# Row-Winograd convolution with max pool on Trainium2: last product in halves, stores image by image, and a new order

## The chip, the cores and the metric

The kernel runs on one core of a Trainium2 chip. The metric is the device time of one execution in microseconds (us), as the median of several runs. A core has five engines that run their own instruction streams and wait for each other by semaphores: TensorE (PE in the profile) for matrix products, VectorE (DVE), ScalarE (ACT), GpSimd (POOL) and SyncE (SP), which here only issues transfers. Sixteen DMA engines move data between the memory outside the core (DRAM) and the core's own memory (SBUF). Products are gathered in PSUM, which the kernel uses as eight banks.

## The reference, cut to what matters

```python
batch, c_in, h, w, c_out, k = 16, 64, 64, 64, 128, 3      # all float32
conv[b, co] += weight[co, ci, kh, kw] * x_pad[b, ci, kh:kh+h, kw:kw+w]   # pad 1, all ci, kh, kw
output[b, c, i, j] = max(conv[b, c, 2*i:2*i+2, 2*j:2*j+2])               # 16 x 128 x 32 x 32
```

A 3x3 convolution with padding 1, followed by a 2x2 maximum without overlap.

## The kernel before, in words

**The algorithm.** Each pooled row needs two rows of the convolution. The four input rows that they read are combined along the row axis, so that the two convolution rows are a + c and b + c with a common part c, and max(a + c, b + c) = max(a, b) + c. So c, the last product of every step, is added after the row maximum has been taken. The taps of the weights are combined the same way into seven blocks (`D2`, `G0`, `D0`, `G2`, `GM`, `G1`, `GP`), which are transposed once at the start.

**The tiling.** There are 32 steps. A step is two images (one on each half of the 128 partitions, numbered h = 0 and 1) and a quarter of the rows: 8 pooled rows of 64 columns for each image, which is 512 numbers on each of 128 output channels, one PSUM bank. The string `TYPES` gives each step one of two forms. A K step reads bf16 rows that a load on GpSimd's queue has cast (`kx`); it has the products PA1, PA2, PB1, PB2 and, last, PR. A W step reads fp32 rows (`wx`, loaded by SP) from which row differences E (`we`) and D (`wd`) and row sums WS (`ws`) are computed on POOL or DVE; it has the products P2, P0, P3 and, last, P1. A product has three matmuls, one for each column tap, for each image; `product` (line 272) collects the two images in `lanes` and emits their matmuls by turns. All emit from line 219 or, for the transposes, line 170.

**The steps between.** The code names them in the order string, each with the step and the image:
- SE, `seed` (copy at line 451, ACT): copies the first sum into the bank of the second, which then goes on from it.
- EV, `evac` (lines 439 and 441, ACT): moves the first sum to SBUF.
- MX, `rowmax` (line 467, DVE): maximum of the two rows, in PSUM. The last product (PR or P1) waits for it.
- OD, `odd` (line 471, ACT): copies the odd columns to SBUF after the last product.
- CM, `colmax` (line 477, DVE): maximum of even and odd columns into the output tile `o` (eight buffers); it gives the PSUM bank back.
- ST, `store` (lines 485 and 487): one store of 256 KB for both images on SP; for step 31 one store for each image, the first on ACT's queue.
- XC, `odd_rows` (line 335, ACT): puts odd rows of a W step into PSUM, so that WS reads them there (line 339). Other WS are a plain sum (line 360) or a reduction (line 352), by the step's place in `SUM_BY_REDUCTION`.
- E, `we` (line 372): on DVE for the steps in `DIFF_ON_VECTOR`, otherwise on POOL. D, `wd` (line 381): on POOL. KS (line 320): row sums of a K step, DVE.
- L (line 112, SP) and LK (line 101, POOL) are loads. LB is a load like L that is held until an earlier operation on DVE is done. The names of weights' blocks with T (transposes on PE) and V (copy of the transposed block to SBUF, on ACT for those in `TURNED_BY_SCALAR`, otherwise on DVE).
- The first K step and the first W step are in two row halves: F and G for their products, SEa/SEb, Ea/Eb, Da/Db; XOa, XOb, XEa, XEb cast the first rows, X1 and X2 the next.

**The order.** Nothing is scheduled by a planner. The string `ORDER` (lines 537 to 591) lists all steps of all engines, and a loop calls them one after the other; each engine executes its own in that order and the semaphores follow from the data. Banks are taken from a list `free` and given back to it in the same order, so the string also decides which bank a step gets. SP's transfers stand in this order too: a transfer that waits holds the ones behind it.

Of the kernel before, what the change touches and what calls it, by code (L numbers as in the profile page):

```python
# [11 lines left out]
def kernel(  # L12
# [460 lines left out]
    def colmax(s, h):  # L473
        if s not in ot:
            ot[s] = o_pool.tile([128, 2, R, WO], FP32, name="o")
        t = tb.pop((s, h))
        nc.vector.tensor_tensor(out=ot[s][:, h], in0=acc[t][:, :, 0::2], in1=od[s, h], op=MAX)  # L477
        free.append(t)

    def store(s, h=None):  # L480
        p, q = place[s]
        dst = out[2 * p : 2 * p + 2, :, q * R : (q + 1) * R, :].rearrange("b c h w -> c b (h w)")
        src = ot[s].rearrange("p b h w -> p b (h w)")
        if h is None:
            nc.sync.dma_start(out=dst, in_=src)
        else:
            (nc.scalar, nc.sync)[h].dma_start(out=dst[:, h : h + 1], in_=src[:, h : h + 1])

# [45 lines left out]
    for m in PRODUCTS:  # L534
# [18 lines left out]
        PA1.13.1 OD.8.1 PA2.13.1 L.19 EV.9.0 SE.11.0 CM.8.1 EV.13.1 L.24 D.12 P0.9.1 OD.8.0 P3.9.1 P2.12.1
        P0.11.0 P3.11.0 WS.11 PA1.10.1 PA2.10.1 MX.9.0 P1.9.0 EV.9.1 PA1.13.0 EV.11.0 ST.4 CM.8.0 XC.14 ST.2
        MX.9.1 OD.9.0 SE.12.1 MX.11.0 P1.9.1 P2.11.1 WS.14 PA2.13.0 P1.11.0 EV.10.1 P0.12.1 EV.13.0 PA1.10.0
        E.14 OD.9.1 CM.9.0 P2.14.0 OD.11.0 SE.11.1 WS.12 CM.9.1 EV.12.1 P3.12.1 P0.11.1 D.14 PB1.10.1 CM.11.0
        E.15 P3.11.1 PA2.10.0 E.19 SE.14.0 EV.11.1 P2.12.0 KS.10 MX.12.1 E.17 PB2.10.1 L.23 P1.12.1 P0.14.0
        SE.12.0 MX.11.1 P1.11.1 P3.14.0 EV.14.0 XC.22 MX.14.0 EV.10.0 P0.12.0 WS.22 P2.14.1 MX.10.1 ST.1 P3.12.0
        E.20 EV.12.0 P1.14.0 OD.14.0 MX.12.0 PB1.13.1 OD.12.1 OD.11.1 PB1.10.0 CM.14.0 PB2.10.0 ST.6 P1.12.0
        CM.12.1 PB2.13.1 E.16 CM.11.1 PR.10.1 SE.14.1 P0.14.1 PA1.21.0 MX.13.1 ST.11 XC.17 PR.13.1 OD.12.0  # L560
        OD.10.1 P3.14.1 EV.14.1 PA2.21.0 MX.10.0 OD.13.1 CM.12.0 P2.15.1 EV.21.0 PR.10.0 D.15 D.16 P2.15.0
        CM.10.1 WS.17 CM.13.1 PA1.18.0 MX.14.1 PA2.18.0 OD.10.0 SE.15.0 P2.16.1 CM.10.0 WS.16 WS.15 P0.15.0
        SE.15.1 P3.15.0 SE.16.1 P1.14.1 PB1.13.0 EV.18.0 P0.15.1 OD.14.1 EV.15.0 P0.16.1 P3.15.1 KS.18 EV.15.1
        LK.2.0 CM.14.1 P2.16.0 ST.12 MX.15.0 ST.14 MX.15.1 P3.16.1 D.17 P2.17.1 EV.16.1 P1.15.1 PB2.13.0 MX.16.1
        SE.16.0 SE.17.1 P1.16.1 P1.15.0 P0.17.1 OD.15.0 P0.16.0 L.28 L.25 MX.13.0 P3.17.1 OD.15.1 EV.16.0
        PR.13.0 PA1.18.1 OD.16.1 P3.16.0 OD.13.0 D.20 WS.20 CM.15.1 EV.17.1 PA2.18.1 P2.17.0 CM.16.1 MX.16.0
        SE.17.0 P2.20.1 CM.13.0 P2.19.0 MX.17.1 EV.18.1 P1.17.1 P1.16.0 P0.17.0 CM.15.0 P3.17.0 OD.16.0 SE.20.1
        PA1.21.1 PB1.18.0 EV.17.0 SE.19.0 CM.16.0 ST.9 WS.19 OD.17.1 D.19 P0.20.1 EV.20.1 PA2.21.1 PB2.18.0
        MX.17.0 MX.18.0 E.24 P0.19.0 E.22 P3.20.1 P1.17.0 P2.19.1 EV.21.1 EV.19.0 CM.17.1 PR.18.0 PB1.18.1 E.23
        P3.19.0 MX.20.1 OD.17.0 OD.18.0 P2.20.0 ST.8 P1.20.1 SE.19.1 WS.23 OD.20.1 CM.17.0 P2.23.0 CM.18.0  # L570
        PB2.18.1 MX.19.0 SE.20.0 P1.19.0 L.30 P0.19.1 MX.18.1 EV.19.1 D.23 P3.19.1 OD.19.0 CM.20.1 KS.21 P0.20.0
        D.22 PR.18.1 P2.22.1 SE.23.0 P3.20.0 ST.10 CM.19.0 MX.19.1 PB1.21.1 EV.20.0 MX.20.0 OD.18.1 P0.23.0
# [65 lines left out]
```

## Time and profile before

| | |
|---|---|
| median of 3 runs | 104.52 us (104.48, 104.52, 104.57) |
| the profiled execution | 104.47 us; its span in the trace 102.7 us |
| granted clock of TensorE | 1.0 throughout |
| PE busy | 96.2 us, 94% of the span |
| DVE busy | 91.6 us, 89% |
| ACT busy | 85.5 us, 83% |
| POOL busy | 77.9 us, 76% |
| moved by DMA | 23.60 MB: 17.14 MB read and 8.39 MB written in DRAM |

The span is what the profile shows between the first and the last instruction; the execution's own time is 1.81 us longer. The costliest groups after the matmuls are the row differences D on POOL (2360 ns each), the row maxima on DVE (691 ns each, 64 of them), the seeds and evacuations on ACT (591 to 614 ns) and the column maxima on DVE (416 ns, 64 of them).

A line of the page's section 5 gives the line of code, the engine, the operation, the tiles, their shape and the count, and then the busy time with the mean of one. A name with q behind an engine (SPq) is its queue, which waits and issues. In section 2 each digit is a tenth of the busy share in one fortieth of the span.

### The profile page before, as it was taken

How to read it: one execution, taken by the hardware profiler on the slowest of the kernel's cores; microseconds unless marked ns; L12 is line 12 of the kernel's file. 1: busy time of each engine (PE TensorE's matmuls, PEld its weight loads, DVE VectorE, ACT ScalarE, POOL GpSimd, SP SyncE). 2: the span in 40 equal slices, each digit the busy share in tenths (PEclk: the TensorE clock that was granted, in tenths of full speed). 3: DMA queues.
4: the chain of work that ended last, by engine and by line, in shares of the span. 5: the costliest groups of instructions: out<-in, count | busy, mean ns of one | idle time of the engine just before them, and what ended most of it. 6: DMA issues, size and time to landing. Idle time of an engine off the chain costs nothing.

```text
span 102.7 us, 2522 instructions
## 1 busy us (share of the span) xinstructions
PE 96.2 (94%) x905; PEld 54.3 (53%) x905; DVE 91.6 (89%) x176; ACT 85.5 (83%) x192; POOL 77.9 (76%) x66
## 2 busy tenths in 40 slices
PE   6969999999999999999999999999999999999920
PEld 2355465444454447655655555567657765555500
DVE  1576979999999999999999989999999999899960
ACT  4278697999889999997998899897989899897830
POOL 6262889995998799489959999789999688990000
PEclk9999999999999999999999999999999999999999
DMA  2989999999999999600538989930803673386553
GB/s 53 286 295 333 281 325 360 362 421 410 293 311 410 311 308 396 220 6 0 175 57 119 245 259 404 389 111 0 307 3 112 216 165 113 106 295 222 208 192 114
DMA packets 13341, 23.60 MB, mean 230 GB/s; under 512 B 1040, under 2 KB 9360, under 8 KB 13328
## 3 DMA queue, kind: packets, MB, share of 16 engines
q1 hardware_dynamic: 12464, 21.20, 58.8%
q0 software_dynamic: 720, 2.10, 11.6%
q8 instruction: 7, 0.11, 0.5%
q10 hardware_dynamic: 144, 0.13, 0.4%
q14 instruction: 6, 0.05, 0.1%
HBM read 17.14 MB, written 8.39 MB: 249 GB/s over the span
## 4 chain that ended last, share of the span: by engine, by line
PE 88%; DMA 4%; DVE 2%; SPq 1%; issue 1%; ACT 0%; DVEq 0%
PE acc L219 86%; DMA kfirst<-in_x_dram 4%; DVE o L477 1%; PE acc L170 1%; DVE acc L467 1%; PE acc L460 1%; SPq L119 0%; ACT kx L492 0%; SPq L115 0%; DVEq L633 0%
## 5 line engine op out<-in xcount | busy, mean ns | idle before, releaser
L219 PEld LDWEIGHTS <-wt 64*128 64x128 bf16 x870 | 51.7, 94 | 39.0 <-issue 2.0
L219 PE MATMUL acc<-wd,wt 64*128 64x504 bf16 (+3 forms) x276 | 54.4, 367 | 0.0
L381 POOL TENSOR_TENSOR wd<-wx 128x1024 bf16<-128x1024 f32 x21 | 49.2, 2360 | 4.5 <-DVE ws L360 2.0
L219 PE MATMUL acc<-kx,wt 64*128 64x504 bf16 (+6 forms) x264 | 44.7, 355 | 0.9 <-DVE wq L508 0.7
L467 DVE TENSOR_TENSOR acc<-acc,ev 128x512 f32<-128x512 f32 x64 | 42.0, 691 | 1.2 <-ACT ev L441 0.7
L219 PE MATMUL acc<-we,wt 64*128 64x512 bf16 (+3 forms) x138 | 32.5, 367 | 0.0
L219 PE MATMUL acc<-ws,wt 64*128 64x512 bf16 (+1 forms) x132 | 32.5, 377 | 0.0
L441 ACT ACTIVATE ev<-acc 128x512 f32<-128x512 f32 x44 | 26.3, 614 | 1.8 <-PE acc L219 1.3
L451 ACT COPY acc<-acc 128x512 f32<-128x512 f32 x42 | 24.5, 591 | 3.0 <-PE acc L219 1.8
L477 DVE TENSOR_TENSOR o<-acc,od 128x256 f32<-128x256 f32 x64 | 24.7, 416 | 0.9 <-ACT od L471 0.9
L471 ACT COPY od<-acc 128x256 f32<-128x256 f32 x64 | 22.8, 382 | 2.2 <-PE acc L219 1.7
L372 POOL TENSOR_TENSOR we<-wx 128x512 bf16<-128x512 f32 x16 | 20.1, 1272 | 4.0 <-PE acc L219 2.4
L219 PE MATMUL acc<-ks,wt 64*128 64x504 bf16 (+1 forms) x60 | 13.7, 377 | 0.0
L439 ACT COPY ev<-acc 128x512 f32<-128x512 f32 x20 | 11.7, 593 | 1.3 <-PE acc L219 1.2
L352 DVE TENSOR_REDUCE ws<-wx 128x512 bf16<-128x1024 f32 x9 | 11.1, 1232 | 0.0
L360 DVE TENSOR_TENSOR ws<-wx 128x512 bf16<-128x512 f32 x7 | 5.3, 766 | 0.0
L320 DVE TENSOR_TENSOR ks<-kx 128x512 bf16<-128x512 bf16 x10 | 4.3, 435 | 0.0
L408 POOL TENSOR_TENSOR wd<-wx 128x512 bf16<-128x512 f32 x2 | 2.5, 1264 | 2.2 <-DVE we L393 2.2
L339 DVE TENSOR_TENSOR ws<-wx,acc 128x512 bf16<-128x512 f32 x6 | 4.1, 675 | 0.0
L595 PE MATMUL acc<-const-bfloat16-1.0 128*128 128x512 bf16 x8 | 3.3, 582 | 0.8 <-PEq L619 0.8
L335 ACT COPY acc<-wx 128x512 f32<-128x512 f32 x6 | 3.6, 598 | 0.1
L372 DVE TENSOR_TENSOR we<-wx 128x512 bf16<-128x512 f32 x4 | 2.9, 749 | 0.3 <-DMA wx<-in_x_dram 0.3
(33 smaller groups left out, 26.6 us busy)
## 6 DMA issues: line engine op xcount, KB each, us to landing
out_dram<-o SPq DMA_DIRECT2D x31, 256.0 KB, 2.9
wx<-in_x_dram SPq DMA_DIRECT2D x10, 512.0 KB, 10.6
wx<-in_x_dram SPq DMA_DIRECT2D x6, 480.0 KB, 9.7
wx<-in_x_dram SPq DMA_DIRECT2D x5, 544.0 KB, 8.5
kx<-in_x_dram POOLq DMA_DIRECT2D x2, 528.0 KB, 7.5
ksecond<-in_x_dram SPq DMA_DIRECT2D x1, 512.0 KB, 6.4
...
```

The source lines that it names most:

```text
L219: nc.tensor.matmul(acc[t][:, i0:i1, o0:o1], wt[lo : lo + CI, tap_of(m0, kw, h), :], rows(lo, i0, i1, c0, c1), start=start and kw == 1, sto ...
L320: nc.vector.tensor_tensor(out=row["ks", s], in0=t[:, f : f + 2 * R : 2, :], in1=t[:, f + 1 : f + 2 * R : 2, :], op=ADD)
L352: nc.vector.tensor_reduce(out=row["ws", s], in_=t[:, f : f + 2 * R, :].rearrange("p (r two) w -> p r w two", two=2), axis=mybir.AxisListTy ...
L360: nc.vector.tensor_tensor(out=row["ws", s], in0=t[:, f : f + 2 * R : 2, :], in1=t[:, f + 1 : f + 2 * R : 2, :], op=ADD)
L372: inst = (nc.vector if vector else nc.gpsimd).tensor_tensor(out=row["we", s], in0=t[:, f : f + 2 * R : 2, :], in1=t[:, f + 1 : f + 2 * R : ...
L381: nc.gpsimd.tensor_tensor(out=row["wd", s], in0=t[:, f + 1 : f + 1 + 2 * R, :], in1=t[:, f - 1 : f - 1 + 2 * R, :], op=SUB)
L439: nc.scalar.copy(out=ev[s, h], in_=acc[t])
L441: nc.scalar.mul(ev[s, h], acc[t], -1.0)
L451: nc.scalar.copy(out=acc[t], in_=acc[ta[s, h]])
L467: nc.vector.tensor_tensor(out=t, in0=t, in1=ev[s, h], op=MAX)
L471: nc.scalar.copy(out=od[s, h], in_=acc[tb[s, h]][:, :, 1::2])
L477: nc.vector.tensor_tensor(out=ot[s][:, h], in0=acc[t][:, :, 0::2], in1=od[s, h], op=MAX)
```

## The change

Five things are changed.

1. **The last product of step 31 in row halves.** New steps H.0 and H.1 do P1 of step 31 for both images, first four pooled rows, then the other four; OD and CM of step 31 are in the same halves. H.0 waits for the row maxima of both images.
2. **Stores of step 31 in three parts:** "a" the upper half of the rows of both images (SP), "b0" the lower half of image 0 (ACT's queue), "b1" of image 1 (SP).
3. **Stores image by image** (two of 128 KB on SP, in place of one of 256 KB) for steps 26 to 30 and for 8, 10, 12, 14, 16 and 20.
4. **Engines of some small steps:** E of steps 9 and 19 goes to POOL and E of step 14 to DVE; other steps use the reduction or the odd rows in PSUM; two casts of taps (g1, g2) go from DVE to ACT, one cast of rows (XEb) from ACT to DVE, the sum GP from POOL to DVE; of the transposed blocks D0, G2, G1 and GP are copied on ACT, where before G0, GM, G1 and GP were.
5. **The order string** is new over its whole length. In the head, TD0 stands before F.0.0 and TG2 before F.0.1, G.0.1 stands behind PA2.2, and the load of step 4 (LB.4) stands behind LB.6. In the tail the column maxima of steps 30 and 29 come before the four half ones of step 31.

```diff
-    DIFF_ON_VECTOR = (3, 8, 9, 15, 19,)
+    DIFF_ON_VECTOR = (3, 8, 14, 15,)
-    SUM_BY_REDUCTION = (1, 3, 11, 12, 19, 20, 24, 28, 31,)
-    ODD_ROWS_IN_PSUM = (4, 6, 8, 14, 17, 22,)
-    TURNED_BY_SCALAR = ("G0", "GM", "G1", "GP",)
-    CAST_BY_SCALAR = ("XEa", "XOa", "XEb", "XOb",)
-    TAPS_BY_VECTOR = ("g1", "g2",)
-    SUMS_BY_GPSIMD = ("GP",)
+    SUM_BY_REDUCTION = (1, 3, 11, 15, 16, 22, 28, 30,)
+    ODD_ROWS_IN_PSUM = (6, 8, 9, 14, 17, 19,)
+    TURNED_BY_SCALAR = ("D0", "G2", "G1", "GP",)
+    CAST_BY_SCALAR = ("XEa", "XOa", "XOb",)
+    TAPS_BY_VECTOR = ()
+    SUMS_BY_GPSIMD = ()
...
+    def last_product(part):
+        span = (0, R // 2) if part == 0 else (R // 2, R)
+        pair_of_taps(tb, N - 1, GP, step1(row["ws", N - 1]), False, None, span)
...
+    def odd_part(s, h, part):
+        if part == 0:
+            od[s, h] = od_pool.tile([128, R, WO], FP32, name="od")
+        nc.scalar.copy(out=part_of(od[s, h], part), in_=part_of(acc[tb[s, h]], part)[:, :, 1::2])
...
     def store(s, h=None):
         p, q = place[s]
...
+        rows = slice(q * R, (q + 1) * R)
+        images = slice(0, 2)
+        if s == N - 1:
+            rows = slice(q * R, q * R + R // 2) if h == "a" else slice(q * R + R // 2, (q + 1) * R)
+            images = slice(0, 2) if h == "a" else slice(int(h[1]), int(h[1]) + 1)
+        elif h is not None:
+            images = slice(int(h), int(h) + 1)
+        dst = out[2 * p : 2 * p + 2, :, rows, :].rearrange("b c h w -> c b (h w)")[:, images]
+        src = ot[s][:, images, rows.start - q * R : rows.stop - q * R].rearrange("p b h w -> p b (h w)")
+        (nc.scalar if h == "b0" else nc.sync).dma_start(out=dst, in_=src)
...
     ORDER = """
-        g0 D2 TD2 XOa g2 GS TG0 VD2 D0 XOb XEb TG2 g1 F.0.0 F.0.1 TD0 uG1 GM VG0 GP XEa F.1.0 F.1.1 VD0 F.2.0
-        uGM EV.0.1 TG1 F.2.1 uGP LB.3 VG2 LK.0.0 TGM X1 LB.4 F.3.0 TGP X2 KS.0 L.11 PA1.2.0 LB.6 Ea F.3.1 VGM
-        LB.9 PA1.2.1 KS.2 EV.0.0 VG1 PA2.2.1 Eb LB.8 MX.0.1 Da G.0.0 MX.0.0 G.0.1 VGP PR.0.1 SEa.1 SEa.0 Db
+        g0 D2 g2 TD2 TG0 D0 XOa GS XOb g1 VD2 TD0 VD0 uG1 XEb F.0.0 TG2 VG0 F.0.1 LB.3 XEa F.1.0 GP F.1.1 TG1
+        VG2 F.2.0 EV.0.0 GM X1 uGM KS.0 LB.6 X2 uGP F.2.1 LB.4 LK.0.0 TGM F.3.1 F.3.0 TGP EV.0.1 VGM Ea MX.0.0
+        Da MX.0.1 PA1.2.0 PA2.2.0 PA1.2.1 G.0.0 VGP VG1 SEa.1 SEa.0 PA2.2.1 Eb G.0.1 PR.0.0 WS.1 L.16 SEb.0
...
-        OD.2.0 EV.3.0 ST.0 CM.2.0 PR.2.1 OD.1.1 E.4 CM.1.0 MX.3.0 P1.3.1 PA1.5.1 PA1.5.0 L.15 PB1.5.0 PA2.5.1
+        SE.3.1 P0.3.1 E.4 SE.3.0 P0.3.0 EV.3.1 MX.2.1 MX.2.0 P3.3.1 OD.1.0 MX.3.1 PR.2.1 P3.3.0 P1.1.1 PR.2.0
+        EV.3.0 CM.1.0 OD.2.1 D.4 XC.6 CM.2.1 PA1.5.0 OD.1.1 PA2.5.0 MX.3.0 L.14 E.6 P1.3.1 CM.1.1 OD.2.0 CM.2.0
+        P2.4.1 OD.3.1 E.11 PA1.5.1 CM.3.1 P1.3.0 EV.5.0 WS.6 ST.0 P2.4.0 OD.3.0 SE.4.1 LK.1.0 PB1.5.0 CM.3.0
...
+        EV.6.0 MX.7.0 ST.1 E.9 PR.7.0 PR.7.1 SE.8.1 L.19 OD.7.1 D.11 P0.6.1 L.22 OD.7.0 P3.6.1 CM.4.0 P0.8.1
...
-        MX.29.1 MX.31.0 MX.31.1 OD.30.0 CM.30.0 OD.30.1 PR.29.0 P1.31.0 PR.29.1 CM.30.1 ST.23 OD.29.0 P1.31.1
-        ST.30 OD.29.1 CM.29.0 OD.31.0 CM.29.1 OD.31.1 ST.29 CM.31.0 ST.31.0 CM.31.1 ST.31.1
+        MX.31.1 ST.27.0 OD.30.0 PR.29.1 PR.29.0 CM.30.1 OD.29.1 H.0 ST.24 OD.29.0 CM.30.0 ST.30.1 CM.29.1 H.1
+        ST.30.0 OD.31.1.0 CM.29.0 CM.31.1.0 OD.31.0.0 ST.29.1 OD.31.0.1 CM.31.0.0 OD.31.1.1 ST.29.0 CM.31.0.1
+        CM.31.1.1 ST.31.a ST.31.b0 ST.31.b1
     """
```

More of the change, by code (lines that the diff above doesn't have):

```diff
@@ L467, in rowmax, with odd, colmax @@
         nc.vector.tensor_tensor(out=t, in0=t, in1=ev[s, h], op=MAX)
-    def odd(s, h):
+    def odd(s, h, part=None):
+        if part is not None:
+            return odd_part(s, h, part)
         od[s, h] = od_pool.tile([128, R, WO], FP32, name="od")
         nc.scalar.copy(out=od[s, h], in_=acc[tb[s, h]][:, :, 1::2])
-    def colmax(s, h):
+    def colmax(s, h, part=None):
+        if part is not None:
+            return colmax_part(s, h, part)
         if s not in ot:
@@ L478, in colmax, with part_of, colmax_part @@
         free.append(t)
+    def part_of(t, part):
+        return t[:, R // 2 * part : R // 2 * (part + 1)]
+    def odd_part(s, h, part):
+        if part == 0:
+            od[s, h] = od_pool.tile([128, R, WO], FP32, name="od")
+        nc.scalar.copy(out=part_of(od[s, h], part), in_=part_of(acc[tb[s, h]], part)[:, :, 1::2])
+    def colmax_part(s, h, part):
+        if s not in ot:
+            ot[s] = o_pool.tile([128, 2, R, WO], FP32, name="o")
+        nc.vector.tensor_tensor(
+            out=part_of(ot[s][:, h], part),
+            in0=part_of(acc[tb[s, h]], part)[:, :, 0::2],
+            in1=part_of(od[s, h], part),
+            op=MAX,
+        )
     def store(s, h=None):
         p, q = place[s]
[L482 to L487, printed above, removed]
+        rows = slice(q * R, (q + 1) * R)
[8 more added lines that the diff above has]
+        (nc.scalar if h == "b0" else nc.sync).dma_start(out=dst, in_=src)
     def cast_rows(n, lo, hi):
@@ L527 @@
         "SE": seed, "EV": evac, "MX": rowmax, "OD": odd, "CM": colmax,
-        "XC": odd_rows, "ST": store,
+        "XC": odd_rows, "H": last_product, "ST": store,
     }
@@ L553 @@
[L553 to L572, printed above, removed]
@@ new lines @@
+        P2.4.1 OD.3.1 E.11 PA1.5.1 CM.3.1 P1.3.0 EV.5.0 WS.6 ST.0 P2.4.0 OD.3.0 SE.4.1 LK.1.0 PB1.5.0 CM.3.0
+        PA2.5.1 KS.5 KS.7 PB1.5.1 LK.1.1 EV.5.1 PB2.5.0 PA1.7.0 SE.4.0 XC.9 WS.4 L.12 P0.4.1 PA2.7.0 PB2.5.1
+        P3.4.1 MX.5.0 P0.4.0 PR.5.0 EV.4.1 D.6 WS.9 PA1.7.1 EV.7.0 MX.4.1 XC.8 PA2.7.1 EV.4.0 MX.5.1 P1.4.1
+        P3.4.0 EV.7.1 OD.5.0 OD.4.1 P2.6.0 E.8 PB1.7.0 MX.4.0 L.17 CM.5.0 CM.4.1 PR.5.1 L.15 PB1.7.1 OD.5.1
+        P1.4.0 PB2.7.0 D.8 CM.5.1 D.9 PB2.7.1 WS.8 SE.6.0 P2.6.1 P0.6.0 OD.4.0 P2.8.1 SE.6.1 P3.6.0 MX.7.1
@@ new lines @@
+        EV.6.0 MX.7.0 ST.1 E.9 PR.7.0 PR.7.1 SE.8.1 L.19 OD.7.1 D.11 P0.6.1 L.22 OD.7.0 P3.6.1 CM.4.0 P0.8.1
+        P3.8.1 MX.6.0 P2.8.0 P1.6.0 P2.9.1 EV.6.1 CM.7.1 P2.9.0 SE.8.0 CM.7.0 P0.8.0 EV.8.1 MX.6.1 OD.6.0 MX.8.1
+        CM.6.0 SE.9.0 P3.8.0 P0.9.0 EV.8.0 SE.9.1 P1.6.1 P1.8.1 OD.6.1 E.12 P2.11.0 P0.9.1 EV.9.0 ST.5 WS.11
+        OD.8.1 P3.9.1 MX.8.0 P3.9.0 SE.11.0 PA1.10.1 CM.6.1 CM.8.1 EV.9.1 P1.8.0 MX.9.0 MX.9.1 D.12 PA2.10.1
+        P0.11.0 XC.14 P1.9.0 PA1.13.1 OD.8.0 CM.8.0 EV.11.0 PA2.13.1 OD.9.0 E.14 P3.11.0 ST.8.0 ST.8.1 PA1.13.0
@@ new lines @@
+        ST.2 EV.10.1 P2.12.1 P1.9.1 CM.9.0 MX.11.0 EV.13.1 WS.14 P2.11.1 SE.12.1 P0.12.1 D.14 WS.12 PA2.13.0
+        EV.13.0 OD.9.1 KS.10 P1.11.0 P3.12.1 ST.6 SE.11.1 OD.11.0 E.15 CM.9.1 PA1.10.0 EV.12.1 CM.11.0 P0.11.1
+        P3.11.1 P2.14.0 PA2.10.0 E.19 MX.12.1 P1.12.1 KS.13 WS.22 SE.14.0 P2.14.1 EV.11.1 P2.12.0 P3.14.0
+        SE.12.0 E.16 EV.10.0 OD.12.1 P0.14.0 PB1.10.1 L.20 PB2.10.1 P0.12.0 MX.11.1 D.15 P3.12.0 EV.14.0
+        PB1.10.0 CM.12.1 EV.12.0 MX.14.0 P1.11.1 PB1.13.1 D.16 P1.14.0 PB2.10.0 MX.12.0 PB2.13.1 P1.12.0 OD.11.1
@@ new lines @@
+        MX.10.1 OD.14.0 L.23 CM.11.1 SE.14.1 ST.11 PA1.21.0 CM.14.0 MX.10.0 PR.10.1 PR.10.0 E.17 P0.14.1 P3.14.1
+        MX.13.1 XC.17 D.17 PR.13.1 ST.4 P2.15.1 OD.10.1 P2.16.1 OD.12.0 CM.10.1 EV.14.1 E.20 CM.12.0 PA2.21.0
+        OD.10.0 WS.17 CM.10.0 P2.15.0 EV.21.0 OD.13.1 SE.15.0 ST.10.0 ST.10.1 MX.14.1 E.22 PA1.18.0 CM.13.1
+        SE.15.1 P1.14.1 SE.16.1 PA2.18.0 EV.18.0 P3.15.0 WS.15 P0.15.0 OD.14.1 L.24 P0.15.1 D.19 P2.16.0 EV.15.1
+        WS.16 CM.14.1 ST.12.0 ST.12.1 P0.16.1 EV.16.1 PB1.13.0 P3.15.1 PB2.13.0 P3.16.1 SE.16.0 P0.16.0 MX.15.1
@@ new lines @@
+        ST.3 MX.16.1 P2.17.1 EV.15.0 P1.15.1 D.20 SE.17.1 P3.16.0 P1.16.1 MX.15.0 OD.15.1 MX.13.0 P1.15.0
+        P0.17.1 CM.15.1 PA1.18.1 EV.16.0 P3.17.1 OD.16.1 OD.15.0 PR.13.0 ST.14.0 ST.14.1 OD.13.0 MX.16.0 CM.15.0
+        EV.17.1 P2.17.0 ST.9 LK.2.0 P1.16.0 PB1.18.0 CM.16.1 CM.13.0 PA2.18.1 SE.17.0 P0.17.0 P2.20.1 P2.19.0
+        MX.17.1 OD.16.0 EV.18.1 P1.17.1 CM.16.0 P3.17.0 SE.20.1 KS.18 PB2.18.0 WS.23 PA1.21.1 ST.15 WS.20 E.23
+        EV.17.0 OD.17.1 P0.20.1 SE.19.0 P3.20.1 EV.20.1 CM.17.1 L.25 MX.17.0 P0.19.0 XC.19 PA2.21.1 E.24 EV.19.0
@@ new lines @@
+        SE.23.1 P2.22.0 P3.22.1 PB2.21.0 SE.22.0 L.30 CM.23.0 PR.21.1 ST.17 L.28 P2.24.0 OD.21.1 MX.22.1 D.25
+        P0.22.0 CM.21.1 P3.22.0 P0.23.1 P3.23.1 MX.21.0 P1.22.1 EV.23.1 PR.21.0 E.25 MX.23.1 SE.24.0 EV.22.0
+        P2.24.1 P1.23.1 OD.22.1 ST.19 OD.21.0 P0.24.0 CM.22.1 P3.24.0 SE.24.1 OD.23.1 P2.25.1 E.27 P0.24.1
+        EV.24.0 CM.21.0 P3.24.1 SE.25.1 P0.25.1 PA1.26.0 MX.22.0 P1.22.0 L.31 P3.25.1 PA2.26.0 EV.24.1 CM.23.1
+        OD.22.0 EV.26.0 WS.24 WS.25 MX.24.1 P2.25.0 P1.24.1 EV.25.1 PA1.26.1 PB1.26.0 P2.27.1 SE.25.0 CM.22.0
@@ new lines @@
+        P2.30.0 ST.27.1 PA1.29.1 CM.26.1 PA2.29.1 EV.28.1 P1.27.0 P2.30.1 E.31 MX.28.0 OD.27.0 PA1.29.0 MX.28.1
+        P1.28.1 ST.20.0 ST.20.1 CM.27.0 P1.28.0 WS.31 SE.30.0 P0.30.0 KS.29 ST.26.1 EV.29.1 OD.28.0 SE.30.1
+        P2.31.1 PA2.29.0 CM.28.0 OD.28.1 EV.30.0 P2.31.0 EV.29.0 P3.30.0 D.31 CM.28.1 P0.30.1 ST.7 EV.30.1
+        P3.30.1 PB1.29.0 PB1.29.1 WS.30 MX.30.0 MX.30.1 ST.28.0 PB2.29.0 SE.31.0 P0.31.0 PB2.29.1 MX.29.0
+        SE.31.1 P0.31.1 P3.31.1 P3.31.0 MX.29.1 ST.28.1 P1.30.0 EV.31.0 P1.30.1 EV.31.1 ST.25 MX.31.0 OD.30.1
@@ L601 @@
         name, *args = s.split(".")
-        steps[name](*map(int, args))
+        steps[name](*(int(a) if a.isdigit() else a for a in args))
 _INS = ['x', 'weight', 'pool_size']
```

39 lines of the change are left out of this document (12 added, 27 removed).

## The prediction, made before the changed kernel was run

> **What bounds the kernel now.** I read the page first: busy shares, the slices over time, the chain that ended last.
>
> ```profile
> span 102.7 us, 2522 instructions
> ...
> PE 96.2 (94%) x905; PEld 54.3 (53%) x905; DVE 91.6 (89%) x176; ACT 85.5 (83%) x192; POOL 77.9 (76%) x66
> ...
> DMA  2989999999999999600538989930803673386553
> ...
> PE 88%; DMA 4%; DVE 2%; SPq 1%; issue 1%; ACT 0%; DVEq 0%
> ```
>
> TensorE (PE) carries 88% of the chain, and VectorE (DVE) has only 5% less to do. The 16 DMA engines are full for the first 40 us, and only then loosely filled. The chain of waits in order of time gives the places:
>
> ```profile
> 1.65 4.30 DMA kfirst<-in_x_dram
> 5.95 0.02 issue
> 5.98 0.41 ACT kx L492
> ...
> 12.27 84.18 PE acc L219 x785
> 96.45 0.04 issue
> 96.50 0.69 DVE acc L467
> ...
> 98.09 0.75 DVE o L477 x2
> 98.83 0.33 DVEq L633
> ```
>
> So there are three regions. A **head**: the first image rows land and ScalarE (ACT) casts them, a chain of 4.7 us. A **middle**: 84.18 us of PE without a break in the chain. A **tail**: the last row maximum and column maxima, then the last store. PE does one product for both images (six matmuls) each 0.648 us; against that pitch the single records show 0.097 us lost at 51.82, 0.096 at 73.23 and 0.137 before the last product. Thus nothing in the middle gains by being faster, except those 0.19 us; anything late there costs in full. The tail is best seen in the traffic of 93 to 103 us (each number is 0.25 us):
>
> ```profile
> GB/s 271 74 0 0 123 373 369 148 25 315 365 381 381 389 279 0 0 0 0 0 0 0 0 324 393 369 356 393 389 377 381 164 0 0 0 0 0 0 0 0
> ```
>
> PE ends at 97.88, yet no byte moves from 96.75 to 98.75; then the last three steps, 768 KB, go out without a gap until 100.97. The last store lands 0.55 us after its last packet (101.52), and 1.12 us of end checks follow. The end is a backlog of stores that began late.
>
> The profiled run took 104.47 us, 1.81 more than its span (102.66), and lies 0.05 under the median (104.52). I sum on the span, then add 1.81 and 0.05.
>
> **PE's own work.** The products stand slot for slot nearly as before; the halved last product adds 6 matmuls with half the columns each: 0.02 us of fixed time.
>
> **Head.** Before, PE does F.0.0 at 5.76, then waits for the second cast (ends 6.38): F.0.1 at 6.43, four transposes TD0 at 6.87, F.1.0 at 7.22. After, TD0 stands ahead of F.0.0, where PE is idle, and TG2 between F.0.0 and F.0.1, in the wait. I rebuilt the slots from the intervals of before (0.26 to 0.33 for a half product, 0.43 to a group of transposes, 0.27 to 0.36 behind it): F.1.0 comes at 6.88, a lead of 0.35. But G.0.1 now stands behind a full product (12.18 against 11.24), so its seeds on ACT (0.59 for a whole one) end at 13.34 and G.1.1, otherwise ready at 13.16, waits to 13.39: 0.23 of the lead goes. Net −0.12; bounds 0 and −0.35. ACT's head gains two casts of taps (0.53 each) and loses one of rows; its last cast still ends before its product by these sums.
>
> **Middle, DVE and ACT.** DVE loses the difference of step 9 (0.749), a reduction for a plain sum (1.232 against 0.766) and two tap casts (0.488 each), and gets XEb and one turn-out back: about 1.2 us less. All this lies beside PE. Row maxima end 0.04 to 0.4 us ahead of their products before, and 0.4 to 2 us earlier after, by sums of rows in the new order. The two old stalls should go: −0.19. New tight places by the same sums: P0.9.1 needs SE.9.1 (ends 34.85 against a slot at 34.84), PA1.10.1 needs the bank that CM.6.1 frees, now behind WS.11 (reduction, pitch 1.15) and MX.8.0: 0.2 together. P0.15.1 needs SE.15.1: 0.1 to 0.19, taken 0.1. The moved XC.9 and XC.19 (0.598 each) replace XC.4 and XC.22 on ACT.
>
> **Middle, GpSimd (POOL).** It loses GP's sum (0.685) and gets E.9 (1.272). That one lies behind a chain that the head sets. Before, the load of step 4 is second of its group (issued 6.96, landed 15.01) and step 11's third (7.44, 17.18). After, L.4 stands behind L.3 and L.6, so it takes the third place: about 17.1, and E.4, which could have begun at 16.37 after D.3, waits for it. From the rows (E 1.272, D 2.35 pitch, 0.57 for each issue of LK.1):
>
> ```profile
> 14.01 4.67 POOL L381 TENSOR_TENSOR wd<-wx 128x1024 bf16<-128x1024 f32 x2 [0.46 <-DVE we L372]
> 18.64 3.73 POOL L372 TENSOR_TENSOR we<-wx 128x512 bf16<-128x512 f32 x3
> ...
> 24.29 7.00 POOL L381 TENSOR_TENSOR wd<-wx 128x1024 bf16<-128x1024 f32 x3 [1.40 <-DVE ws L360]
> ```
>
> E.4 ends 18.4, D.4 20.7, E.6 22.0, E.11 23.2, both LK.1 24.3, D.6, D.8 and D.9 31.3, E.9 about 32.5. P2.9.0 reads E.9 in the slot that began at 32.25 before, 32.13 with the lead: a stall of 0.4, after which the places at P0.9.1 and PA1.10.1 have their 0.2 of slack back. If the load lands by 16.4 there is no stall; each us beyond 17.1 costs a us. I take 0.4, with 0.2 as the value without it (the two places then count).
>
> **Stores in the middle.** Twelve more issues on SP (0.33 to 0.43 each, SP idle most of the time). Where a store waits on SP for its column maximum, the loads behind it wait too; the loads left from 45 us on land 4 us or more ahead of their readers, so nothing: bounds 0 and 0.2.
>
> **Tail.** The order is CM.30.1, CM.30.0, CM.29.1, CM.29.0, then four half column maxima. DVE's pitch is 0.331 for 256 columns, 0.267 of it proportional, so a half costs 0.198 and the split adds 2 × 0.064 = 0.13; the last ends near 99.3 against 99.16. The first of the six stores no longer waits for both images: issued 97.43 against 97.86. Then 97.78, 98.10, 98.42, 98.87 (both images, upper half), 99.02 and 99.33. Bytes begin 0.89 after an issue: 98.32. A packet of 1024 B took 46 ns in the DMA records, 2048 B 84 and 4096 B 159; extended, 512 B take 27. Image stores of 128 KB then take 0.37, the upper half 0.43, the last two 0.22 each. Without gaps that would end before 100.3; but the last issue cannot start moving before 100.22, and the upper half's not before 99.76: the last packet leaves about 100.67 with the two 64 KB stores sharing engines. Landing 101.22, against 101.52. The end checks run through the queues' semaphores in turn; the last store's is now the last checked, not followed by four of 0.06: −0.25. Tail: −0.55. Bounds −0.1 (512 B packets as dear as 1024 B, checks unchanged) and −0.65.
>
> A cost fit in the Trainium skill, DMA: Bandwidth & Descriptors, section "Anatomy of one DMA — SWDGE (gpsimd) path", speaks against the split: about 2.0 us fixed for each DMA plus the bytes over 436 GB/s; its section "Measured (HBM→SBUF, 128 partitions, SWDGE, issued from GpSimd)" asks for batches of 1 MiB. By it the 64 KB store would land 2.15 us after its issue, at 101.48, and the tail would gain 0.3 with the checks. Here a whole 256 KB store that found the engines free landed in 2.08 us (issued 89.49), where the fit says 2.60, so the trace disagrees with the fixed part.
>
> **Sum.** −0.12 − 0.19 + 0.4 + 0.1 + 0.02 = +0.21 to the end of PE; −0.55 behind it: −0.34. Span 102.32, profiled run 104.13, median 104.18.
>
> **Rivals.** (a) *Clean middle*: L.4 lands by 16.4 and the sums overstate stalls (applied to before they do by 0.08 each). Then PE ends 0.1 to 0.25 early and the total is 103.7 to 103.95. For it: before, nearly every such place held. (b) *Given back*: the last store lands a fixed time after its issue and no backlog is saved, since 99.33 is later than 99.19; before that took 2.33, so it lands at 101.66, and with the sum to the end of PE the median is 104.6 with the saving in the checks, 104.85 without, and 104.4 if part of the backlog is saved. The packets' row speaks against it. That the page's rule is right (above) falls in here, at 104.4. (c) *Slower*: POOL becomes the bound near 32 us. In the crowded first 40 us, loads of 512 to 544 KB take 8.5 to 10.6 us (medians of the page); from an issue near 8.6 that is 17.1 to 19.2. Each us of L.4 goes through E.4, D.4, the three D and E.9 into P2.9.0, with PE standing idle. From about 17.6 on (stall 0.9) the tail's gain is eaten; at 18.2 to 19.2 the stall is 1.5 to 2.5, 1.1 to 2.1 more than in the sum, and the run takes 105.3 to 106.3. Against it: the three loads that end with L.4 carry 1536 KB, the three that ended with L.11 carried 1568. (d) *No effect of the split*: the last two stores are issued on two queues 0.3 apart, and the schedule may leave ACT's behind SP's; this costs 0.1 at most and is inside the bounds.
>
> **How the numbers follow.** A difference of 0.21 us (0.2%) is about what a measurement of this kernel can tell from none. The forecast, 104.0 to 104.3, has 0.42; (a), below 104.0, 0.15; (b), 104.3 to 104.75, 0.18; (c), above 104.75, 0.25, which takes in any other queue that is late the same way: lateness costs in full, while earliness gains nothing. Faster is the first two, 0.57. Same is (b), 0.18. The range 103.7 to 105.0 cuts off a half of (c) and the edge of (a). The likeliest case's own range is 104.0 to 104.3.
>
> **What would show it.** Right: F.1.0 near 6.88; E.4 on POOL at 17.1 and E.9 ending near 32.5, with an idle PE of about 0.4 before P2.9.0; no loss at 51.8 and 73.2; first of the last stores issued near 97.4 plus PE's shift; traffic beginning 0.4 us sooner and landing 0.55 us after the last packet. Wrong: an idle PE above 1 us in 30 to 37 us, or any other stretch of PE's chain broken (then DVE or ACT appears in it); a last store that lands over 2.2 us after its issue; a half column maximum above 0.3 us.

## The result and the profile after

| | median us | lowest to highest | runs |
|---|---|---|---|
| before | 104.54 | 103.98 to 106.76 | 22 |
| changed | 105.38 | 104.24 to 108.03 | 22 |

The ratio is 1.005 (95% interval 1.003 to 1.0071): about 0.5 us slower, where 104.18 and a gain of 0.34 were forecast. A ratio, here and below, leaves out slow runs, those over 1.5% above the fastest of their kernel (the 106.53 us execution profiled here is one), while a median is of all runs. The median lies outside the range of 103.7 to 105.0. A second set of runs gave 1.0049 (1.0023 to 1.0075). The span of the profiled execution is 104.74 us; a second profile, of a 105.30 us execution (called "changed again"), stands beside it below.

First the page of the changed kernel (span, busy times, shares of the chain).

```profile
span 104.7 us, 2555 instructions
...
PE 97.4 (93%) x911; PEld 58.7 (56%) x911; DVE 92.1 (88%) x177; ACT 85.9 (82%) x195; POOL 78.9 (75%) x66
...
PE 86%; DMA 5%; DVE 3%; ACT 1%; SPq 1%; issue 0%; DVEq 0%
```

VectorE's share of the chain has risen from 2% to 3%. Where, the chain in order of time says (start, length, what):

```profile
1.65 4.86 DMA kfirst<-in_x_dram
...
12.04 13.06 PE acc L219 x132
25.10 0.03 issue
25.13 0.02 DVEq L471
25.15 0.67 DVE ws L364
25.82 0.61 DVE acc L471
26.43 0.59 DVE ws L343
27.02 0.62 DVE acc L471
27.64 0.04 issue
27.68 71.52 PE acc L219 x657
```

Before, PE ran 84.18 us without a break. Here it hands the chain to VectorE at 25 us: row sums and row maxima come too late. The cause stands just ahead of that, in VectorE's line of time, beside GpSimd's (start, length, engine and operation, count):

```profile
22.22 0.42 DVE L485 TENSOR_TENSOR o<-acc,od 128x256 f32<-128x256 f32 x1
22.55 2.67 DVE L324 TENSOR_TENSOR ks<-kx 128x512 bf16<-128x512 bf16 x2
25.14 0.68 DVE L364 TENSOR_TENSOR ws<-wx 128x512 bf16<-128x512 f32 x1
```

```profile
14.24 2.35 POOL L385 TENSOR_TENSOR wd<-wx 128x1024 bf16<-128x1024 f32 x1 [0.51 <-issue]
18.70 1.27 POOL L376 TENSOR_TENSOR we<-wx 128x512 bf16<-128x512 f32 x1 [2.10 <-DMA wx<-in_x_dram]
19.93 2.36 POOL L385 TENSOR_TENSOR wd<-wx 128x1024 bf16<-128x1024 f32 x1
22.24 2.70 POOL L376 TENSOR_TENSOR we<-wx 128x512 bf16<-128x512 f32 x2
24.88 1.10 POOL L101 DMA_DIRECT2D kx<-in_x_dram  x2
```

Before, KS.5 and KS.7, two additions, took 0.42 us each, and GpSimd's three E (18.64 to 22.38, in the prediction's lines) had ended ahead of them:

```profile
22.85 0.75 DVE L320 TENSOR_TENSOR ks<-kx 128x512 bf16<-128x512 bf16 x2
```

Here they take 2.67 us together (1.25 and 1.49 singly, overlapping a little). Meanwhile GpSimd does E.6 (22.24 to 23.52) and E.11 (23.47 to 24.94). KS.5 ends at 23.80 and KS.7 at 25.22: each 0.28 us after GpSimd's operation. GpSimd is there so late because E.4 waited 2.10 us for the load of step 4.

The tail, the traffic from 96 to 106 us (0.25 us a number; PE ends at 99.89):

```profile
GB/s 360 365 352 41 16 86 385 393 217 20 25 25 25 0 0 0 0 131 361 168 365 160 361 156 352 316 346 226 207 0 0 0 0 0 0 0 0 0 0 0
```

The unbroken block of 350 to 390 GB/s is gone: at first every other number is less than half of its neighbours, so the DMA engines idle in part between one store and the next. SP's line says why:

```profile
99.54 2.87 SPq L517 DMA_DIRECT2D out_dram<-o  x6
```

Six issues take 2.87 us, 0.48 for each. They start 0.43, 0.47, 0.51, 0.50 and 0.50 apart, although the column maxima that they wait for ended 0.33, 0.33, 0.33, 0.52 and 0.40 apart.

To compare profiles, the spans are cut at four points: the landing of the first image's lower rows (the second `kfirst` transfer), the start of slots 24 and 60 of PE (counted from 0; a slot is the matmuls of one product, or the transposes of one block of the weights), and its last matmul. In every kernel the same amount of PE work lies between them, within 0.04 us.

| kernel | landing | to slot 24 | 24 to 60 | 60 to end of PE | to end of span | KS.5, KS.7 |
|---|---|---|---|---|---|---|
| before | 5.95 | 8.87 | 23.26 | 59.79 | 4.78 | 0.42, 0.42 |
| changed | 6.51 | 8.60 | 25.02 | 59.76 | 4.85 | 1.25, 1.49 |
| changed again | 6.76 | 8.60 | 23.52 | 59.77 | 4.85 | 0.90, 0.41 |

The landing is not set by the order (below); the rest is the kernel: −0.27 in the head, +0.26 to +1.76 in slots 24 to 60, −0.03 to the end of PE, +0.07 in the tail.

### The profile page after: what moved, and what is told of

It reads as the page before. It is cut to its first block, busy times and chain, and to the rows that moved or that the text cites. A ratio compares the mean times of both kernels' runs of the same rounds, so it can differ in the third digit from the quotient of the medians.

```text
span 104.7 us, 2555 instructions
## 1 busy us (share of the span) xinstructions
PE 97.4 (93%) x911; PEld 58.7 (56%) x911; DVE 92.1 (88%) x177; ACT 85.9 (82%) x195; POOL 78.9 (75%) x66
## 4 chain that ended last, share of the span: by engine, by line
PE 86%; DMA 5%; DVE 3%; ACT 1%; SPq 1%; issue 0%; DVEq 0%
PE acc L219 85%; DMA kfirst<-in_x_dram 5%; DVE acc L471 1%; PE acc L170 1%; DVE ws L364 1%; ACT od L494 1%; DVE ws L343 1%; PE acc L464 1%; DVE o L499 0%; SPq L119 0%; ACT kx L521 0%; SPq L115 0%; DVEq L664 0%; DVEq L471 0%
## 5 line engine op out<-in xcount | busy, mean ns | idle before, releaser
L219 PEld LDWEIGHTS <-wt 64*128 64x128 bf16 x876 | 56.1, 94 | 36.8 <-issue 4.8
L219 PE MATMUL acc<-kx,wt 64*128 64x504 bf16 (+5 forms) x264 | 46.5, 355 | 1.0 <-ACT kx L521 0.9
L471 DVE TENSOR_TENSOR acc<-acc,ev 128x512 f32<-128x512 f32 x64 | 42.5, 692 | 2.0 <-PE acc L219 0.9
L219 PE MATMUL acc<-ws,wt 64*128 64x512 bf16 (+3 forms) x138 | 33.0, 367 | 0.2 <-DVE acc L471 0.2
L219 PE MATMUL acc<-we,wt 64*128 64x512 bf16 (+3 forms) x138 | 32.5, 367 | 0.0
L376 POOL TENSOR_TENSOR we<-wx 128x512 bf16<-128x512 f32 x17 | 21.7, 1289 | 5.5 <-DMA wx<-in_x_dram 2.1
L485 DVE TENSOR_TENSOR o<-acc,od 128x256 f32<-128x256 f32 x62 | 24.1, 416 | 1.4 <-ACT od L477 1.1
L219 PE MATMUL acc<-ks,wt 64*128 64x504 bf16 (+1 forms) x60 | 14.3, 376 | 0.8 <-DVE acc L471 0.8
L356 DVE TENSOR_REDUCE ws<-wx 128x512 bf16<-128x1024 f32 x8 | 9.8, 1230 | 0.0
L324 DVE TENSOR_TENSOR ks<-kx 128x512 bf16<-128x512 bf16 x10 | 6.4, 652 | 0.2 <-ACT kx L521 0.2
L101 POOL DMA_DIRECT2D kx<-in_x_dram x5 | 2.9, 590 | 0.2 <-issue 0.2
```

Of the source, the lines that this page charges most:

```text
L219: nc.tensor.matmul(acc[t][:, i0:i1, o0:o1], wt[lo : lo + CI, tap_of(m0, kw, h), :], rows(lo, i0, i1, c0, c1), start=start and kw == 1, sto ...
L324: nc.vector.tensor_tensor(out=row["ks", s], in0=t[:, f : f + 2 * R : 2, :], in1=t[:, f + 1 : f + 2 * R : 2, :], op=ADD)
L356: nc.vector.tensor_reduce(out=row["ws", s], in_=t[:, f : f + 2 * R, :].rearrange("p (r two) w -> p r w two", two=2), axis=mybir.AxisListTy ...
L376: inst = (nc.vector if vector else nc.gpsimd).tensor_tensor(out=row["we", s], in0=t[:, f : f + 2 * R : 2, :], in1=t[:, f + 1 : f + 2 * R : ...
L471: nc.vector.tensor_tensor(out=t, in0=t, in1=ev[s, h], op=MAX)
```

## The experiments

The theory after the first comparison: **pile-up**. The load of step 4, moved behind that of step 6, lands 2.3 to 3.6 us later, GpSimd runs late, and KS.5 and KS.7 fall beside its operations on SBUF and don't get on. (Before, it landed at 15.01.) For the tail: **issue**. SP's time for each store takes the place of the DMA engines' backlog.

**Load of step 4 back in its place** (changed kernel):

```diff
-        ... F.0.1 LB.3 XEa ... F.2.1 LB.4 LK.0.0 ...
+        ... F.0.1 LB.3 LB.4 XEa ... F.2.1 LK.0.0 ...
```

> The changed kernel with one load moved: step 4's rows are issued right behind step 3's, as before the change (there they landed at 15.0 us). Pile-up theory: in the changed kernel's profile this load landed at 18.6, so E.4 began at 18.7 instead of 16.6, GpSimd was 2 us late, and the bf16 row sums KS.5 and KS.7 on VectorE fell beside E.6 and E.11 on GpSimd and took 1.25 and 1.49 us instead of 0.42. With the load back, E.4 should begin by 16.7, E.11 end by about 23, KS.5 take at most 0.7 and KS.7 about 0.42, the stalls of 1.0 and 0.44 us ahead of PR.5 and P1.4.1 shrink to under 0.3, and the time fall by 0.7 to 1.2 us, to 104.2 to 104.7. Rival, E.9: the delay comes from E.9 on GpSimd alone, then the two stalls stay as they are and the time stays near 105.4. Rival, chance: the first image rows landed 0.56 late in that one profile; then nothing changes but scatter.

104.76 us median against 105.18 of the kernel before on that chip; ratio 0.9982 (0.9953 to 1.0011), where the changed kernel has 1.005: 0.7 us less, the low end of what was expected. The load landed at 14.33 us, and GpSimd:

```profile
14.11 2.35 POOL L385 TENSOR_TENSOR wd<-wx 128x1024 bf16<-128x1024 f32 x1 [0.51 <-issue]
16.43 1.26 POOL L376 TENSOR_TENSOR we<-wx 128x512 bf16<-128x512 f32 x1
17.65 2.36 POOL L385 TENSOR_TENSOR wd<-wx 128x1024 bf16<-128x1024 f32 x1
19.97 2.52 POOL L376 TENSOR_TENSOR we<-wx 128x512 bf16<-128x512 f32 x2
```

The wait of 2.10 is gone, E.11 ends at 22.49, KS.5 and KS.7 take 0.42 and 0.41 (22.42 to 23.17), and no stall over 0.06 us is left between 24 and 28 us. One moved load (step 6's rows go one place back for it) is worth the loss and a little more.

**The collision made in the kernel before**, by moving KS.5 and KS.7 on VectorE beside E.6:

```diff
-        OD.3.0 WS.6 EV.5.1 PB1.5.1 E.6 CM.3.0 WS.4 PA2.7.0 SE.4.1 EV.5.0 PB2.5.1 KS.5 KS.7 SE.4.0 WS.9 P0.4.1
+        OD.3.0 E.6 KS.5 KS.7 WS.6 EV.5.1 PB1.5.1 CM.3.0 WS.4 PA2.7.0 SE.4.1 EV.5.0 PB2.5.1 SE.4.0 WS.9 P0.4.1
```

> The kernel before with KS.5 and KS.7 moved on VectorE ahead of WS.6, so that they start near 21.3 us while GpSimd does E.6 (21.1 to 22.4); nothing else moves. Pile-up theory (a bf16 row sum on VectorE does not get on while GpSimd works on SBUF): KS.5 takes 1.0 to 1.4 us, ending about 0.3 after E.6, KS.7 about 0.42; VectorE is 0.7 to 1.0 us late into MX.5 and PE loses 0.3 to 0.9 us ahead of PR.5; time 104.8 to 105.4. Rival (these sums were slow in the changed kernel because their rows or their semaphores were late): both take 0.42 here, VectorE only changes its order, PE loses nothing, 104.5.

106.42 against 105.18, ratio 1.0071 (1.0031 to 1.0111): 0.75 us for two additions moved ahead of three other operations of VectorE, with everything else as before. The two sums on VectorE and the three E on GpSimd:

```profile
23.98 1.32 DVE L320 TENSOR_TENSOR ks<-kx 128x512 bf16<-128x512 bf16 x2
```

```profile
20.94 3.74 POOL L372 TENSOR_TENSOR we<-wx 128x512 bf16<-128x512 f32 x3
24.64 0.57 POOL L101 DMA_DIRECT2D kx<-in_x_dram  x1
```

KS.5 takes 0.99 and ends at 24.97, 0.28 after E.6 (24.68). KS.7, beside a DMA issue of GpSimd, takes 0.41. PE loses 0.92 us once. (All times in this execution, of 108.07 us, lie 2.3 us later, since the rows landed at 7.23 and the granted clock was 0.81 from 6 to 15 us.)

**E.9 back on VectorE** (changed kernel; the sums of step 9 plain again):

```diff
-    DIFF_ON_VECTOR = (3, 8, 14, 15,)
-    ODD_ROWS_IN_PSUM = (6, 8, 9, 14, 17, 19,)
+    DIFF_ON_VECTOR = (3, 8, 9, 14, 15,)
+    ODD_ROWS_IN_PSUM = (6, 8, 14, 17, 19,)
-        ... PA1.7.0 SE.4.0 XC.9 WS.4 ...
+        ... PA1.7.0 SE.4.0 WS.4 ...
```

> The changed kernel with E.9 back on VectorE and the sums of step 9 plain (no XC.9), as before the change. Rival of the prediction (GpSimd late through E.9 into P2.9): PE no longer waits near P2.9 and the time falls by 0.4 us or more. Pile-up theory: P2.9 waited 0.08 us at most in the changed kernel, so the time stays within 0.2 us of the changed kernel's and KS.5 and KS.7 are as slow as there whenever E.4 starts after 17.2.

Neither: 107.98 against 105.03, ratio 1.0258 (1.0213 to 1.0304). I had not seen that the copy XC.9 was a protection. VectorE and GpSimd:

```profile
25.30 0.69 DVE L471 TENSOR_TENSOR acc<-acc,ev 128x512 f32<-128x512 f32 x1
25.90 2.58 DVE L364 TENSOR_TENSOR ws<-wx 128x512 bf16<-128x512 f32 x1
```

```profile
25.55 2.37 POOL L385 TENSOR_TENSOR wd<-wx 128x1024 bf16<-128x1024 f32 x1
28.55 4.67 POOL L385 TENSOR_TENSOR wd<-wx 128x1024 bf16<-128x1024 f32 x2 [0.64 <-DVE ws L364]
```

WS.9, with both operands in SBUF, took 2.58 us and ended 0.56 after D.6 (27.91). In the changed kernel the same sum, with its odd rows in PSUM, took 0.67 beside D.6. PE lost 2.3 us there. So it is not the bf16 type. The ten profiles agree without an exception: wherever a sum or difference of VectorE with both operands in SBUF (128x512) began with 0.2 us or more of a GpSimd operation on SBUF still to go, it ended 0.28 to 0.29 us after that operation when its operands were bf16, and 0.55 to 0.56 us after it when they were fp32. As a test of E.9 the run is spoilt in its time. P2.9 waited 0.08 us in the changed kernel and not at all in "changed again"; that does not clear E.9, as shown under the slower rival below.

**The changed kernel again**, unedited, on the same chip as the one with E.9 and the last two below.

> The changed kernel once more, unchanged, on the same chip as the three kernels beside it, to have its time against theirs and another profile. Pile-up theory: its time against the kernel before is again about 1.005, and in the profile the start of E.4 decides: where E.4 begins after 17.2, one or both of KS.5 and KS.7 take over 1.2 us beside E.6 and E.11 and PE loses 0.4 to 1.5 us between 24 and 28 us; where it begins earlier neither happens. Tail: last issue on SP again 2.0 to 2.1 us behind the end of PE. Rival, E.9: PE waits over 0.3 us at P2.9 whatever KS does.

105.46 against 105.03, ratio 1.0049. My threshold was too sharp: E.4 began at 17.37 and E.11 ended at 23.42, so KS.5 (from 22.81) took 0.90 and not 1.2, KS.7 0.41, and PE lost only 0.24 us, at 30 us. P2.9 did not wait. The loss grows with what is left of E.6 and E.11 when KS.5 begins. In the four executions with a profile and the load in third place (the one with whole stores and the one with E.9 among them), the load landed at 17.28, 17.30, 18.18 and 18.63; in second place it landed at 13.79 to 15.17. The load, and no longer the first rows, then sets PE's time: summed from the tables, the two executions with the load at 17.28 and 17.30 reach slot 60 at the same time, 38.88, though their first rows landed 0.44 us apart (6.32 and 6.76), and the one at 18.63 gets there 1.25 us later. With the load back in its place, slot 60 (38.35 and 38.68) follows the first rows (6.38 and 6.68). So this is a likely source of the changed kernel's scatter; the executions without a profile do not show it.

**Stores of steps 30 and 29 whole** (changed kernel):

```diff
-        ... CM.30.0 ST.30.1 CM.29.1 H.1 ST.30.0 ... CM.31.1.0 OD.31.0.0 ST.29.1 ... ST.29.0 ...
+        ... CM.30.0 CM.29.1 H.1 ST.30 ... CM.31.1.0 OD.31.0.0 ... ST.29 ...
```

> The changed kernel with the stores of steps 30 and 29 whole again (one issue each, after both images), all else as changed. Issue theory: SP needs about 0.47 us for each store, so six stores from 99.54 on end with an issue at 101.95, 0.53 behind the last column maximum; with four the last issue comes about 0.1 to 0.2 behind the last column maximum, 0.35 to 0.45 earlier against the end of PE, and the last landing 0.2 to 0.4 earlier against the end of PE (the bytes of the whole stores start later and may hold it back). Time lower by 0.2 to 0.4 us. Rival, small packets: the cost is in the 512 B packets or a fixed cost for each store on the DMA engines; then the last landing stays 3.9 us behind the end of PE.

The time can't tell it (105.56; ratio 1.0042, 1.0008 to 1.0076, against 1.005). The trace does: the last issue comes 1.65 us behind the end of PE, not 2.06, and the last landing 3.66, not 3.94; the end of the span 4.69, not 4.85. The issue theory holds, and small packets do not: the last 64 KB took 1.88 us to land in the changed kernel, 0.01 above its quickest store. This execution, of 105.12 us, shows the collision as well: KS.5 took 1.33 us, and slots 24 to 60 lost 0.70. But 3.66 is still no better than the 3.64 before.

**The changed kernel's tail alone, in the kernel before** (everything from MX.31.0 on, with the changed functions; the middle stores stay whole):

```diff
-        MX.31.0 MX.31.1 OD.30.0 CM.30.0 OD.30.1 PR.29.0 P1.31.0 PR.29.1 CM.30.1 ST.23 OD.29.0 P1.31.1 ST.30 ...
+        MX.31.0 OD.30.1 MX.31.1 OD.30.0 PR.29.1 PR.29.0 CM.30.1 OD.29.1 H.0 ST.23 OD.29.0 CM.30.0 ST.30.1 CM.29.1
+        H.1 ST.30.0 OD.31.1.0 CM.29.0 CM.31.1.0 OD.31.0.0 ST.29.1 OD.31.0.1 CM.31.0.0 OD.31.1.1 ST.29.0 ...
```

> The kernel before with the changed kernel's tail alone: last product, odd copies and column maxima of step 31 in halves, stores of steps 29 and 30 image by image, step 31's in three parts, in the changed kernel's order from MX.31.0 on. Middle stores stay whole. Issue theory: PE ends at 97.9 as before; the first of these stores is issued near 97.45, the last near 99.9 because SP takes 0.47 to 0.5 for each; last landing near 101.8 against 101.5, of which the shorter end checks give back 0.25: the time is the same as before within 0.2 us. Prediction on record: tail 0.55 us shorter, 104.0. Rival, small packets: the last landing comes over 2.2 us after its issue.

105.15 against 105.18, ratio 1.0006 (0.9981 to 1.0031): no effect. Last issue 2.08 and last landing 3.97 behind the end of PE, end of span 4.93 against 4.78. So the whole tail of the change is worth nothing or slightly less than nothing.

**Only step 30's store split, in the kernel before** (ST.23 moved ahead of it, to keep the stores' order):

```diff
-        CM.30.0 OD.30.1 PR.29.0 P1.31.0 PR.29.1 CM.30.1 ST.23 OD.29.0 P1.31.1 ST.30
+        ST.23 CM.30.0 ST.30.0 OD.30.1 PR.29.0 P1.31.0 PR.29.1 CM.30.1 OD.29.0 P1.31.1 ST.30.1
```

> The kernel before with one edit: the store of step 30 image by image, the first one issued after its own column maximum; all else as before. Issue theory: two issues of about 0.45 each fit ahead of step 29's store (its column maxima end at 98.50), so nothing behind them is later; bytes start 0.33 us sooner and the last landing comes 0.1 to 0.25 us earlier against the end of PE (3.64 before). Time 0.1 to 0.25 lower, too little to be told from none. Rival, fixed cost for each store on the DMA engines: last landing 3.64 or more behind the end of PE.

Ratio 0.9981 (0.9951 to 1.0012), not told from none. The trace refutes my expectation: the last landing comes 3.63 behind the end of PE. The traffic from 97 to 105 us (0.2 us a number):

```profile
GB/s 369 297 5 0 0 0 0 0 0 51 358 246 236 364 62 302 379 394 374 384 379 364 41 0 0 0 0 0 0 0 0 0 0 0 0 0 0 0 0 0
```

Step 30's bytes do start sooner, and then the engines idle until step 29's store is issued. By this row, what ends the kernel is that issue and the 512 KB behind it.

**Both findings together** (changed kernel): load of step 4 back, and a tail without halves, with step 31 stored as before the change, step 30 image by image, step 29 whole:

```diff
-        ... MX.31.1 ST.27.0 OD.30.0 PR.29.1 PR.29.0 CM.30.1 OD.29.1 H.0 ST.24 OD.29.0 CM.30.0 ST.30.1 CM.29.1 H.1 ...
+        ... MX.31.1 ST.27.0 OD.30.0 PR.29.1 PR.29.0 CM.30.1 OD.29.1 P1.31.0 P1.31.1 ST.24 OD.29.0 CM.30.0 ST.30.1
+        ST.30.0 CM.29.1 OD.31.0 CM.29.0 OD.31.1 ST.29 CM.31.0 ST.31.0 CM.31.1 ST.31.1
```

> The changed kernel with both findings used: step 4's load right behind step 3's, and a tail with four stores on SP and one on ACT (step 30 image by image, 29 whole, 31 whole images as before the change, no halves). Pile-up theory and issue theory: KS.5 and KS.7 at about 0.42 us, no loss over 0.3 us between 24 and 28 us, last store issued 1.35 us behind the end of PE (2.06 in the changed kernel), last landing about 3.4 behind it (3.94), end of span about 4.5 behind it (4.85). Time 0.8 to 1.3 us under the changed kernel's and 0.3 to 0.6 under the kernel before, ratio 0.994 to 0.997. Rival, small packets and fixed costs on the DMA engines: last landing stays 3.6 to 3.9 behind the end of PE.

104.68 against 105.03, ratio 0.9968 (0.9942 to 0.9994): 0.3% faster than the kernel before, and faster than the changed kernel. The tail came out at 3.61 and 4.64 rather than 3.4 and 4.5; by the row above, the landing could not gain.

The remaining rows of the table:

| kernel | landing | to slot 24 | 24 to 60 | 60 to end of PE | to end of span | KS.5, KS.7 |
|---|---|---|---|---|---|---|
| load 4 back | 6.38 | 8.60 | 23.37 | 59.75 | 4.84 | 0.42, 0.41 |
| both findings | 6.68 | 8.60 | 23.40 | 59.75 | 4.64 | 0.42, 0.42 |
| 30 and 29 whole | 6.32 | 8.60 | 23.96 | 59.75 | 4.69 | 1.33, 0.41 |
| E.9 on VectorE | 6.57 | 8.73 | 26.48 | 59.75 | 4.85 | 0.62, 1.49 |
| before, KS moved | 7.23 | 10.31 | 24.17 | 59.80 | 4.79 | 0.99, 0.41 |
| before, new tail | 6.21 | 8.87 | 23.55 | 59.84 | 4.93 | 0.42, 0.42 |
| before, 30 split | 6.53 | 8.87 | 23.26 | 59.79 | 4.72 | 0.42, 0.42 |

Without the landing, "both findings" is 8.60 + 23.40 + 59.75 + 4.64 = 96.39 against 96.70 before, a ratio of 0.997 on the time, as measured. "Load 4 back" is 96.56, 0.14 under, 0.9987 (measured 0.9982). The changed kernel's two are 96.74 and 98.23, 0.04 and 1.53 over; its median of 0.5 over lies between, and in "changed again" the late first rows hide a part of the loss. "Before, new tail" lost 0.24 us at P2.4 in its one profile, when step 6's rows landed at 20.78 and the copy XC.6 waited for them; its time says that this is not its rule.

## Why the prediction was wrong, step by step

Term by term, as forecast and as measured in "changed again" and in the changed kernel's first profile: the head −0.12, and −0.27 in both; from there to the end of PE +0.33 (−0.19 + 0.4 + 0.1 + 0.02), and +0.24 and +1.73; the tail −0.55, and +0.07 in both. The tail failed by 0.62 us in both. The middle's sum came out near in "changed again", but by luck: another wait stood in the place of the one that was forecast, and the first rows landed late.

**Wrong: VectorE in the middle.** "All this lies beside PE" put KS at its ordinary duration. I had worked out that E.6 ends at 22.0 and E.11 at 23.2 (22.20 and 23.42 in "changed again"), from a load at 17.1 (17.30), and I asked only what this does to E.9 on the same engine. KS.5 and KS.7 stand on VectorE from 22.5 on. Before, E.6 had ended at 22.38 and KS.5 began at 22.85, a margin of 0.47 us. The new order had used up that margin even with the load in its place (KS.5 began 0.07 ahead of the end of E.11 and still took 0.41); the late load then turned it into a collision. One sign that the prediction named for being wrong, VectorE in PE's chain, is what appeared. The price was in the profile before: the plain row sums (smallest, median, largest duration in ns):

```profile
L360 DVE TENSOR_TENSOR ws<-wx x7: 680/684/990, 23.5 to 91.9; 128x512 bf16<-128x512 f32 x7
```

The 990 is WS.30, begun while D.31 had 0.44 us to go. I took the mean of this group, 0.766, as its price, where the scatter was the message. The reductions, one operand, take 1.22 to 1.25 beside GpSimd (WS.3 of the changed kernel lies beside D.3 for its whole 1.231), and sums from PSUM 0.67 to 0.68 throughout.

The Trainium skill, SBUF — State Buffer, section "Who interferes with whom", states this: a VectorE instruction with two SBUF inputs contends with a GpSimd instruction that reads SBUF, over a shared pair of ports that is an exclusive lock, and the order of issue decides who is blocked. The trace agrees: the ends 0.28 and 0.56 us after GpSimd's, whatever the wait. A DMA issue of GpSimd did not block here (KS.7 took 0.41 beside one).

**The slower rival had the right beginning, and its end was hidden.** (c) named the late load, E.4 and GpSimd, with a chance of 0.25, but sent the delay through E.9 into P2.9. P2.9 lost 0.08 us at most; the loss of 0.26 to 1.76 comes earlier and by another way. But the forecast's 0.4 there is not refuted. In "changed again" (E.9, then the first matmul that reads it):

```profile
31.69 1.27 POOL L376 TENSOR_TENSOR we<-wx 128x512 bf16<-128x512 f32 x1
33.02 0.38 PE L219 MATMUL acc<-we,wt 64*128 64x512 bf16 x1
```

E.9 ended at 32.96, near the forecast 32.5, and the matmul began 0.07 us later; where PE did wait for E.9, in the first profile, it began 0.05 us after E.9's end. So E.9 came barely in time, after VectorE had already cost PE 0.24 us and the first rows had landed 0.81 us later than in the profile before. Without the collision PE would have lost about as much at P2.9 (an estimate from these rows: 0.24 less the 0.02 to spare). Both ways start from the load of step 4, moving it back removes both, and no run here parts them: that the load is the cause is shown, and that the collision alone can cost 0.75 us, but not how much would be left of the loss without the collision.

**Wrong: the tail, −0.55 forecast, +0.07 measured.** The last landing came 0.30 us later against the end of PE, where 0.30 earlier was forecast. Two steps failed. The issues were put at the ends of the column maxima, 0.33 apart, but SP needs about 0.48 for each: forecast, from the end of PE, −0.45, −0.10, 0.22, 0.54, 0.99 and 1.45; measured −0.35, 0.08, 0.55, 1.06, 1.56 and 2.06. The profile before had stores in close succession at 89.49, 89.92, 90.42 and 90.97, a pitch of 0.43 to 0.55, and I had set SP's cost in the tail at none. And "a backlog of stores that began late" was wrong: the traffic was gapless, but step 29's store set its end, as the split of step 30 showed. The packets were priced right (512 B took 27 ns, as extended). The end checks came out as forecast: 0.91 us from the last landing to the end of the span (0.87 forecast, 1.14 before). Rival (b), with a chance of 0.18, had the tail nearer: 0.25 saved in the checks and nothing of the backlog; but it, too, had the last issue at 1.45.

**Right, mis-sized: the head.** F.1.0 follows F.0.1 by 0.33, not 0.79, and G.1.1's stall costs 0.20 by slot 24 (0.23 forecast). The net is −0.27, not −0.12: G.0.1's place costs as forecast, but TG2 in the wait before F.0.1 does not push F.0.1 back.

**Right: from slot 60 on.** The two old stalls are gone; PA1.10.1 waits 0.12 to 0.15 in every profile of the new order, P0.15.1 not at all. Net −0.03.

**Wrong: the chances.** A quarter for all lateness was too little, and the range assumed a kernel as steady as the three runs shown. Over 22 runs, the kernel before itself went from 103.98 to 106.76.
